# Log-sum-exp over rows: fewer GpSimd additions in the last rows, an early part of the range check, and other load sizes

## The chip, the cores and the metric

The kernel runs on one core of one Trainium2 chip. The metric is the device time of one execution in microseconds, lower is better. The time before is the median of three runs.

## The reference

For each of 32 x 512 = 16384 rows of 1024 numbers (fp32) the kernel returns the logarithm of the sum of the exponentials:

```python
"x": np.random.randn(32, 512, 1024).astype(np.float32)

def reference(x):
    max_x = np.max(x, axis=-1, keepdims=True)
    return (max_x.squeeze(-1) + np.log(np.sum(np.exp(x - max_x), axis=-1))).astype(np.float32)
```

## The kernel before

Each of the 128 partitions holds NC = 128 rows of 1024 elements. "Row 112" below means row 112 of every partition. The kernel takes the exponentials without the maximum, sums each row into one column of `sumexp`, and takes the logarithm. At the end it checks that all sums lie in a range in which that is exact enough; if they don't, a second path (not taken with these data) does everything again with the maximum.

The work is one long pipeline, written out by hand, with no scheduler: the order of the code is the order of each engine.

- SP issues 18 loads of x into a ring of 48 rows (`load`). A load waits until the sums that still read its place in the ring are done. The sizes and what is done with each load stand in the table `LOADS`: a size in rows, and then a list of parts.
- ScalarE waits for a load (`act.wait(landed[i], 16)`) and takes one exponential, in place, for each part of it.
- The sums of a part are made in one of these ways. **R**: VectorE reduces s whole rows with one `reduce_sum`. **G**: GpSimd adds the second half of each row onto its first half (`tensor_tensor`), and VectorE later reduces the halves (`sum_folded`), half the elements. **T**: VectorE adds both halves of one row and accumulates, one instruction a row (`add_halves`, two inputs). **a** is the first piece of the last row, summed by `add_halves`; **b** is the rest of the last row, which ScalarE itself accumulates while it takes the exponential.
- **H** in the list of parts calls `sum_folded` at once; without it this is done at the end of the load. **L** is the logarithm of the first 112 columns, which SP then stores. So in "G6 R10" VectorE reduces the ten whole rows and then the six half ones.

```python
    (16, "R16"), (16, "R16"), (16, "R16"), (16, "G6 R10"), (15.59375, "R9 G6"),
    ...
    (1.46875, "T1"), (1.0625, "T1"), (0.78125, "T1"), (0.59375, "T1+a"), (0.65625, "b"),
```

Behind the last load two things follow the last sum. On one side ScalarE takes the logarithms of columns 112 to 126 and of the last one, and SP stores these 16 columns. On the other side stands the range check: VectorE compares all 128 columns with the lower bound (`clamped`, `bad`) and sums them (`total`), TensorE adds these up over the partitions into one number (`count`, three products), and VectorE compares this with the upper bound (`fine`). ScalarE and VectorE load that truth value and branch; SP waits for both and for the store.

Of the kernel before, what the change touches and what calls it, by code (L numbers as in the profile page):

```python
# [9 lines left out]
LOW, HIGH = 1e-15, 1e15  # L10
# [4 lines left out]

LOADS = [
# [4 lines left out]
]  # L23


# [23 lines left out]
def kernel(  # L49
# [5 lines left out]
    nc = tc.nc  # L55
# [8 lines left out]
    AX = mybir.AxisListType  # L64
    ALU = mybir.AluOpType
# [4 lines left out]
    NC = n // P  # L70
    H = d // 2
# [8 lines left out]
    def source(e0, size):  # L80
        assert e0 >= W * d or e0 + size <= W * d
        return x_rest[:, e0 - W * d : e0 - W * d + size] if e0 >= W * d else x_rows[:, e0 : e0 + size]
# [4 lines left out]
        ])  # L87
        for size, parts in LOADS
    ]
    assert sum(size for size, _ in loads) == NC * d  # L90

    def sbuf(name, cols, dtype=fp32, rows=P):
        return nc.alloc_sbuf_tensor(name, [rows, cols], dtype).ap()

    ring = sbuf("ring", RING * d)
    sumexp = sbuf("sumexp", NC + 1)
    res = sbuf("res", NC)
    clamped = sbuf("clamped", NC)
    bad = sbuf("bad", 1)
    total = sbuf("total", 1)  # L100
    far = sbuf("far", 1)
    ones = sbuf("ones", 1)
    fine = sbuf("fine", 1, i32, 1)
    count = nc.alloc_psum_tensor("count", [1, 1], fp32).ap()
# [3 lines left out]
    dve = Counted(nc, nc.vector, "dve")  # L108
    pe = Counted(nc, nc.tensor, "pe")
    pool = Counted(nc, nc.gpsimd, "pool")  # L110
# [8 lines left out]
    constants = pool.did(nc.gpsimd.memset(far, 100 * HIGH))  # L119
# [4 lines left out]
    def load(i, here, done_before, size):  # L124
        for a, b, who, at in users:
            if a < here + size and b > here:
                sp.wait(who, at)
        users[:] = [u for u in users if not (u[0] < here + size and u[1] > here)]
        return nc.sync.dma_start(
            out=ring[:, here : here + size], in_=source(done_before, size)  # L130
        ).then_inc(landed[i], 16)

    c = 0
# [7 lines left out]
    def sum_folded():  # L141
        for c0, p0, s, at in folded:
            dve.wait(pool, at)
            half = ring[:, p0 : p0 + s * d].rearrange("p (c d) -> p c d", d=d)[:, :, 0:H]
            at = dve.did(nc.vector.reduce_sum(out=sumexp[:, c0 : c0 + s], in_=half, axis=AX.X))  # L145
            users.append((p0, p0 + s * d, dve, at))
            summed.append((c0, c0 + s, at))
        folded.clear()

    def add_halves(v, col):  # L150
        h = v.shape[-1] // 2
        lo = v[:, 0:h]
        return dve.did(nc.vector.scalar_tensor_tensor(  # L153
            out=lo, in0=lo, scalar=1.0, in1=v[:, h : 2 * h],
            op0=ALU.mult, op1=ALU.add, accum_out=sumexp[:, col : col + 1],
        ))

    for i, (size, parts) in enumerate(loads):
        if here + size > RING * d:
            assert here == p  # L160
            p = here = 0
        dma = load(i, here, done_before, size)
        first_load = first_load or dma.ins
        end = here + size
        done_before += size
        act.wait(landed[i], 16)
        for k, part in enumerate(parts):
            if part[0][0] == "H":
                sum_folded()
                continue  # L170
            if part[0][0] == "L":
                assert c >= W
                act.wait(dve, max(at for c0, _, at in summed if c0 < W))
                ln_early = act.did(nc.scalar.activation(  # L174
                    out=res[:, 0:W], in_=sumexp[:, 0:W], func=AF.Ln
                ))
                continue
            rows = sum(s for how, s in part if how in "RTG")
            more = any(q[0][0] not in "HL" for q in parts[k + 1 :])
            upto = p + rows * d if more else end  # L180
            v = ring[:, here:upto]
            if part[-1][0] == "b":
                last = act.did(nc.scalar.activation(  # L183
                    out=v, in_=v, func=AF.Exp, accum_out=sumexp[:, NC : NC + 1]
                ))
                here = upto
                continue
            at = act.did(nc.scalar.activation(out=v, in_=v, func=AF.Exp))  # L188
            here = upto
            for how, s in part:  # L190
                rows = ring[:, p : p + s * d].rearrange("p (c d) -> p c d", d=d)
                if how == "G":
                    pool.wait(act, at)
                    folded.append((c, p, s, pool.did(nc.gpsimd.tensor_tensor(  # L194
                        out=rows[:, :, 0:H], in0=rows[:, :, 0:H], in1=rows[:, :, H:d], op=ALU.add,
                    ))))
                elif how == "R":
                    dve.wait(act, at)
                    users.append((p, p + s * d, dve, dve.did(nc.vector.reduce_sum(  # L199
                        out=sumexp[:, c : c + s], in_=rows, axis=AX.X  # L200
                    ))))
                    summed.append((c, c + s, dve.n))
                elif how == "T":
                    dve.wait(act, at)
                    for r in range(s):
                        n_sums = add_halves(rows[:, r, :], c + r)
                        users.append((p + r * d, p + (r + 1) * d, dve, n_sums))
                        summed.append((c + r, c + r + 1, n_sums))
                elif how == "a":
                    dve.wait(act, at)  # L210
                    summed.append((LAST, NC, add_halves(ring[:, p:upto], LAST)))
                    s = 0
                c += s
                p += s * d
        sum_folded()
        assert here == end
# [5 lines left out]
    sums = dve.n  # L222
# [4 lines left out]
        out=res[:, LAST:NC], in_=sumexp[:, NC : NC + 1], func=AF.Ln, bias=sumexp[:, LAST:NC]  # L227
# [1 line left out]
    sp.wait(act, ln_last)  # L229
    nc.sync.dma_start(out=out_rest, in_=res[:, W:NC]).then_inc(stored, 16)  # L230

    dve.wait(dve, sums)
    dve.did(nc.vector.scalar_tensor_tensor(  # L233
        out=clamped, in0=sumexp[:, 0:NC], scalar=LOW, in1=sumexp[:, 0:NC],
        op0=ALU.max, op1=ALU.not_equal, accum_out=bad,
    ))
    at = dve.did(nc.vector.reduce_sum(out=total, in_=sumexp[:, 0:NC], axis=AX.X))  # L237
    pe.wait(pool, constants)
    pe.wait(dve, at)
    pe.did(nc.tensor.matmul(count, lhsT=bad, rhs=far, start=True, stop=False))  # L240
    pe.did(nc.tensor.matmul(count, lhsT=ones, rhs=total, start=False, stop=False))  # L241
    pe.wait(act, last)
    at = pe.did(nc.tensor.matmul(  # L243
        count, lhsT=ones, rhs=sumexp[:, NC : NC + 1], start=False, stop=True
    ))
    dve.wait(pe, at)
    at = dve.did(nc.vector.tensor_scalar(out=fine, in0=count, scalar1=HIGH, scalar2=None, op0=ALU.is_lt))  # L247
# [6 lines left out]
    with nc.If(all_fine < 1):  # L254
# [5 lines left out]
        for c0 in range(0, NC, RING):  # L260
# [6 lines left out]
            for c1, c2 in ((c0, edge), (edge, c0 + s)):  # L267
                if c1 == c2:
                    continue
                nc.scalar.dma_start(  # L270
                    out=ring[:, (c1 - c0) * d : (c2 - c0) * d],
                    in_=source(c1 * d, (c2 - c1) * d),
# [4 lines left out]
                out=neg, in_=v, op=ALU.max, axis=AX.X, negate=True  # L277
# [3 lines left out]
                out=v, in0=v, in1=neg[:, :, None].to_broadcast([P, s, d])  # L281
# [5 lines left out]
                out=sumexp[:, c0 : c0 + s], in_=v, axis=AX.X  # L287
# [71 lines left out]
```

## Time and profile before

| | us |
|---|---|
| median of 3 runs | 162.95 (162.81 to 163.07) |
| profiled execution | 163.12 |
| its span in the trace | 161.8 |
| VectorE busy | 116.0 (72%) |
| ScalarE busy | 115.0 (71%) |
| GpSimd busy | 42.3 (26%) |
| load queue's share of the 16 DMA engines' time | 97.0% |

The page shows one profiled execution. In its rows, L188 is ScalarE's exponential, L199 the reduction of whole rows (R), L145 the reduction of halves (after G), L153 the T sum, L194 GpSimd's addition, L233 and L237 the range check on VectorE, L129 the loads. Behind the arrow `<-` in brackets stands what the engine had waited for. A row "x16 | 90.0, 9001 | 42.3" gives the number of instructions, their busy time in us and mean ns, and the engine's idle time before them.

### The profile page before, as it was taken

Reading aid. Unit: us, or ns where it says so; the run is one execution under the profiler, and the core shown is the slowest. Engines: PE = TensorE matmul, PEld = TensorE weight load, DVE = VectorE, ACT = ScalarE, POOL = GpSimd, SP = SyncE. Lnnn points to the kernel's source line nnn. Section 1 sums busy time; section 2 is a strip of 40 time slices with the busy share of each in tenths; the row PEclk is TensorE's granted clock in tenths of the full one; section 3 lists DMA queues with packets and bytes.
Section 4 is the critical chain, followed back from the end, with each engine's and each line's share of the span. In section 5 each row is a group of like instructions: output and inputs, shape, how many; then the busy total and the mean of one; then the engine's idle time right before and its main releaser. Section 6 shows DMA issues by size and latency. Waiting matters only on the chain.

```text
span 161.8 us, 168 instructions
## 1 busy us (share of the span) xinstructions
PE 0.3 (0%) x6; PEld 0.2 (0%) x6; DVE 116.0 (72%) x40; ACT 115.0 (71%) x32; POOL 42.3 (26%) x16
## 2 busy tenths in 40 slices
PE   0000000000000000000000000000000000000000
PEld 0000000000000000000000000000000000000000
DVE  0000000019999499986999679999969999999996
ACT  3000069980899609993299915999998989899994
POOL 0000000000000000000009700002998299299830
DMA  8997997997998999799799598989998999999990
GB/s 292 486 518 308 470 519 324 454 518 340 437 518 356 421 519 437 340 518 454 317 505 505 253 505 370 543 381 424 434 434 356 440 448 412 420 414 427 417 368 3
DMA packets 2880, 67.18 MB, mean 415 GB/s; under 512 B 576, under 2 KB 576, under 8 KB 1344
## 3 DMA queue, kind: packets, MB, share of 16 engines
q1 hardware_dynamic: 2880, 67.18, 97.0%
HBM read 67.11 MB, written 0.07 MB: 415 GB/s over the span
## 4 chain that ended last, share of the span: by engine, by line
DMA 43%; DVE 30%; ACT 24%; POOL 1%; issue 0%; PE 0%
DMA ring<-in_x_dram 43%; ACT ring L188 24%; DVE sumexp L199 23%; DVE sumexp L145 4%; DVE ring L153 3%; POOL ring L194 1%; DVE clamped L233 0%; DVE total L237 0%; PE count L240 0%; DVE fine L247 0%; PE count L243 0%; PE count L241 0%
## 5 line engine op out<-in xcount | busy, mean ns | idle before, releaser
L188 ACT ACTIVATE ring<-ring 128x16384 f32<-128x16384 f32 (+21 forms) x26 | 112.3, 4373 | 42.9 <-DMA ring<-in_x_dram 42.9
L199 DVE TENSOR_REDUCE sumexp<-ring 128x16 f32<-128x16384 f32 (+6 forms) x10 | 90.0, 9001 | 42.3 <-ACT ring L188 42.2
L194 POOL TENSOR_TENSOR ring<-ring 128x3072 f32<-128x3072 f32 (+5 forms) x10 | 41.9, 4211 | 112.2 <-ACT ring L188 112.2
L145 DVE TENSOR_REDUCE sumexp<-ring 128x6 f32<-128x3072 f32 (+5 forms) x10 | 21.2, 2119 | 1.9 <-POOL ring L194 1.9
L153 DVE SCALAR_TENSOR_TENSOR ring<-ring 128x512 f32<-128x512 f32 (+1 forms) x8 | 5.4, 718 | 0.0
L117 ACT ACT_TABLE_LOAD x1 | 1.3, 1283 | 1.4 <-PEq L58 1.4
L183 ACT ACTIVATE ring<-ring 128x672 f32<-128x672 f32 x1 | 0.8, 764 | 0.1
L224 ACT ACTIVATE res<-sumexp 128x15 f32<-128x15 f32 x1 | 0.2, 214 | 0.6 <-DVE ring L153 0.6
L153 DVE DVE_READ_ACCUMULATOR ring<-ring 128x1 f32 x8 | 0.6, 78 | 0.0
L247 DVE TENSOR_SCALAR fine<-count 1x1 int32<-1x1 f32 x1 | 0.1, 147 | 0.5 <-PE count L243 0.5
L240 PE MATMUL count<-far,bad 128*1 128x1 f32 x2 | 0.2, 164 | 160.3 <-DVE total L237 160.3
L118 POOL MEMSET ones<- 128x1 f32 x1 | 0.1, 98 | 1.0 <-POOLq L58 1.0
L240 PEld LDWEIGHTS count<-far,bad 128*1 128x1 f32 x2 | 0.1, 79 | 160.3 <-issue 160.3
L233 DVE SCALAR_TENSOR_TENSOR clamped<-sumexp 128x128 f32<-128x128 f32 x1 | 0.3, 291 | 0.0
L237 DVE TENSOR_REDUCE total<-sumexp 128x1 f32<-128x128 f32 x1 | 0.3, 280 | 0.0
L174 ACT ACTIVATE res<-sumexp 128x112 f32<-128x112 f32 x1 | 0.3, 279 | 0.0
L226 ACT ACTIVATE res<-sumexp 128x1 f32<-128x1 f32 x1 | 0.3, 279 | 0.0
L241 PE MATMUL count<-total,ones 128*1 128x1 f32 x2 | 0.2, 164 | 0.0
L243 PE MATMUL count<-sumexp,ones 128*1 128x1 f32 x2 | 0.2, 162 | 0.0
L183 ACT ACTIVATION_READ_ACCUMULATOR ring<-ring 128x1 f32 x1 | 0.2, 186 | 0.0
L343 POOL MEMSET const-float32-0.0<- 128x1 f32 x1 | 0.1, 99 | 0.2 <-issue 0.2
L241 PEld LDWEIGHTS count<-total,ones 128*1 128x1 f32 x2 | 0.1, 82 | 0.0
(6 smaller groups left out, 0.6 us busy)
## 6 DMA issues: line engine op xcount, KB each, us to landing
ring<-in_x_dram SPq DMA_DIRECT2D x1, 7984.0 KB, 26.4
ring<-in_x_dram SPq DMA_DIRECT2D x1, 5840.0 KB, 20.8
ring<-in_x_dram SPq DMA_DIRECT2D x1, 4480.0 KB, 15.2
ring<-in_x_dram SPq DMA_DIRECT2D x1, 3472.0 KB, 23.3
ring<-in_x_dram SPq DMA_DIRECT2D x1, 2800.0 KB, 20.7
ring<-in_x_dram SPq DMA_DIRECT2D x1, 2080.0 KB, 20.8
ring<-in_x_dram SPq DMA_DIRECT2D x1, 1456.0 KB, 24.0
ring<-in_x_dram SPq DMA_DIRECT2D x1, 1328.0 KB, 26.7
```

The lines of the kernel that those rows point to most:

```text
L117: nc.scalar.preload_act_table_set("natural_log_exp_and_others")
L145: at = dve.did(nc.vector.reduce_sum(out=sumexp[:, c0 : c0 + s], in_=half, axis=AX.X))
L153: return dve.did(nc.vector.scalar_tensor_tensor(out=lo, in0=lo, scalar=1.0, in1=v[:, h : 2 * h], op0=ALU.mult, op1=ALU.add, accum_out=sume ...
L174: ln_early = act.did(nc.scalar.activation(out=res[:, 0:W], in_=sumexp[:, 0:W], func=AF.Ln))
L183: last = act.did(nc.scalar.activation(out=v, in_=v, func=AF.Exp, accum_out=sumexp[:, NC : NC + 1]))
L188: at = act.did(nc.scalar.activation(out=v, in_=v, func=AF.Exp))
L194: folded.append((c, p, s, pool.did(nc.gpsimd.tensor_tensor(out=rows[:, :, 0:H], in0=rows[:, :, 0:H], in1=rows[:, :, H:d], op=ALU.add,))))
L199: users.append((p, p + s * d, dve, dve.did(nc.vector.reduce_sum(out=sumexp[:, c : c + s], in_=rows, axis=AX.X))))
L226: ln_last = act.did(nc.scalar.activation(out=res[:, LAST:NC], in_=sumexp[:, NC : NC + 1], func=AF.Ln, bias=sumexp[:, LAST:NC]))
L233: dve.did(nc.vector.scalar_tensor_tensor(out=clamped, in0=sumexp[:, 0:NC], scalar=LOW, in1=sumexp[:, 0:NC], op0=ALU.max, op1=ALU.not_equal ...
L240: pe.did(nc.tensor.matmul(count, lhsT=bad, rhs=far, start=True, stop=False))
L241: pe.did(nc.tensor.matmul(count, lhsT=ones, rhs=total, start=False, stop=False))
```

## The change

- `LOADS` has other sizes behind row 64, and other parts behind row 48. Loads stay 18, and the ninth still ends at row 112.
- GpSimd's last addition is row 118's. Before, it also added row 122; rows 115 to 117, too, are split differently: before, 115 was an R and 116 and 117 were Gs; after, 114 and 115 are Gs, 116 and 117 Ts. There are ten T sums instead of seven. An H stands in four places, so that sums of halves come ahead of the following R or T.
- A new part **C** sums the folded halves and then checks the columns so far (0 to 113) with `check(0, 0, 114)`: the same two VectorE instructions and two of the three matmuls, now in the tenth load. At the end `check(1, 114, 128)` does the other 14 columns. VectorE comes to it behind the sum of rows 112 and 113 and ahead of that of rows 114 and 115. In its first instruction both inputs are `sumexp`.
- The logarithm L moves from the end of the eleventh load to the end of the twelfth.

```diff
-    (16, "R16"), (16, "R16"), (16, "R16"), (16, "G6 R10"), (15.59375, "R9 G6"),
-    (11.40625, "G5 R7"), (8.75, "G6 R2"), (6.78125, "G3 R4"), (5.46875, "G4 R2"),
-    (4.0625, "G3 R1"), (2.84375, "G2 L"), (2.59375, "G1 T2"), (1.9375, "T1 G1"),
-    (1.46875, "T1"), (1.0625, "T1"), (0.78125, "T1"), (0.59375, "T1+a"), (0.65625, "b"),
+    (16, "R16"), (16, "R16"), (16, "R16"), (16, "G6 H R10"), (14.40625, "R9 G5"),
+    (11.59375, "G3 R5 R4"), (9.3125, "G3 H R6"), (6.875, "G4 R3"), (5.8125, "G2 H R4"),
+    (2.96875, "G2 C"), (3.5, "G2 H T2"), (2.65625, "G1 T2 L"), (1.46875, "T1"),
+    (1.6875, "T2"), (1.28125, "T1"), (0.9375, "T1"), (0.75, "T1+a"), (0.75, "b"),
...
+    def check(k, c0, c1):
+        dve.wait(dve, dve.n)
+        dve.did(nc.vector.scalar_tensor_tensor(
+            out=clamped[:, c0:c1], in0=sumexp[:, c0:c1], scalar=LOW, in1=sumexp[:, c0:c1],
+            op0=ALU.max, op1=ALU.not_equal, accum_out=bad[:, k : k + 1],
+        ))
+        at = dve.did(nc.vector.reduce_sum(
+            out=total[:, k : k + 1], in_=sumexp[:, c0:c1], axis=AX.X
+        ))
+        if k == 0:
+            pe.wait(pool, constants)
+        pe.wait(dve, at)
+        pe.did(nc.tensor.matmul(count, lhsT=bad[:, k : k + 1], rhs=far, start=k == 0, stop=False))
+        pe.did(nc.tensor.matmul(count, lhsT=ones, rhs=total[:, k : k + 1], start=False, stop=False))
...
+            if part[0][0] == "C":
+                sum_folded()
+                checked = c
+                check(0, 0, c)
+                continue
...
-    dve.wait(dve, sums)
-    dve.did(nc.vector.scalar_tensor_tensor(
-        out=clamped, in0=sumexp[:, 0:NC], scalar=LOW, in1=sumexp[:, 0:NC],
-        op0=ALU.max, op1=ALU.not_equal, accum_out=bad,
-    ))
-    at = dve.did(nc.vector.reduce_sum(out=total, in_=sumexp[:, 0:NC], axis=AX.X))
-    pe.wait(pool, constants)
-    pe.wait(dve, at)
-    pe.did(nc.tensor.matmul(count, lhsT=bad, rhs=far, start=True, stop=False))
-    pe.did(nc.tensor.matmul(count, lhsT=ones, rhs=total, start=False, stop=False))
+    check(1, checked, NC)
```

More of the change, by code (lines that the diff above doesn't have):

```diff
@@ L98 @@
     clamped = sbuf("clamped", NC)
-    bad = sbuf("bad", 1)
-    total = sbuf("total", 1)
+    bad = sbuf("bad", 2)
+    total = sbuf("total", 2)
     far = sbuf("far", 1)
@@ L178 @@
             rows = sum(s for how, s in part if how in "RTG")
-            more = any(q[0][0] not in "HL" for q in parts[k + 1 :])
+            more = any(q[0][0] not in "HLC" for q in parts[k + 1 :])
             upto = p + rows * d if more else end
```

## The prediction

> **What bounds the kernel now.** I read the page first, then the chain of waits in order of time, then groups by form for durations, and the timeline behind 138 us.
>
> ```profile
> PE 0.3 (0%) x6; PEld 0.2 (0%) x6; DVE 116.0 (72%) x40; ACT 115.0 (71%) x32; POOL 42.3 (26%) x16
> ...
> DMA 43%; DVE 30%; ACT 24%; POOL 1%; issue 0%; PE 0%
> ```
>
> No engine is full over the span, and the chain has a stretch of each. So what counts is who ends last in which stretch. Stretches by the windows view (columns: PE, PEld, DVE, ACT, POOL busy, clock, DMA share, GB/s), then the chain (start, length, what):
>
> ```profile
> 79.80:138.30 58.50, 0.00 (x0) 0.00 (x0) 54.42 (x9) 51.43 (x10) 28.69 (x5) 1.00 0.98 421
> 138.30:158.20 19.90, 0.00 (x0) 0.00 (x0) 19.73 (x21) 19.47 (x15) 13.26 (x6) 1.00 0.96 400
> ```
>
> ```profile
> 117.62 20.70 DMA ring<-in_x_dram
> ...
> 138.35 11.22 ACT ring L188 x5
> 149.57 0.07 issue
> 149.64 2.37 POOL ring L194
> ...
> 152.03 1.22 DVE sumexp L145
> ```
>
> The loads stream without a pause (share 0.98, then 0.96), so row 112 is in at 138.32 (117.62 + 20.70) and nothing before that can pull the end. From there five exponentials, one GpSimd addition and then VectorE without a gap set the end. In the last 19.9 us VectorE is busy 19.73 and ScalarE 19.47: the tail is balanced and VectorE ends last. Where exactly it ends (timeline; start, length):
>
> ```profile
> 153.16 0.68 DVE L153 SCALAR_TENSOR_TENSOR ring<-ring 128x512 f32<-128x512 f32 x1
> 154.38 0.68 DVE L145 TENSOR_REDUCE sumexp<-ring 128x1 f32<-128x512 f32 x1
> 154.50 1.27 POOL L194 TENSOR_TENSOR ring<-ring 128x512 f32<-128x512 f32 x1 [1.27 <-ACT ring L188]
> 154.98 1.33 DVE L153 SCALAR_TENSOR_TENSOR ring<-ring 128x512 f32<-128x512 f32 x1
> 157.45 0.68 DVE L153 SCALAR_TENSOR_TENSOR ring<-ring 128x512 f32<-128x512 f32 x1
> 158.06 0.68 DVE L153 SCALAR_TENSOR_TENSOR ring<-ring 128x512 f32<-128x512 f32 x1
> 158.19 0.76 ACT L183 ACTIVATE ring<-ring 128x672 f32<-128x672 f32 x1
> 158.86 0.19 ACT L183 ACTIVATION_READ_ACCUMULATOR ring<-ring 128x1 f32 x1
> 159.29 0.33 DVE L153 SCALAR_TENSOR_TENSOR ring<-ring 128x176 f32<-128x176 f32 x1
> 159.66 0.29 DVE L233 SCALAR_TENSOR_TENSOR clamped<-sumexp 128x128 f32<-128x128 f32 x1
> 159.88 0.28 DVE L237 TENSOR_REDUCE total<-sumexp 128x1 f32<-128x128 f32 x1
> 160.08 0.34 SPq L230 DMA_DIRECT2D out_dram<-res  x1
> ```
>
> Three things are to be seen. VectorE ends its last sum at 159.62 (159.29 + 0.33); call this X. ScalarE's last accumulator is out at 159.05, 0.57 earlier. And the T sum at 154.98 took 1.33 instead of 0.68: it ran beside a GpSimd addition (154.50 to 155.77) and ended 0.54 behind that one's end, so it had stood until 156.31 - 0.68 = 155.63. A T sum (two inputs in the ring) waits for a GpSimd addition in flight; the reduction at 154.38, one input, overlaps the same addition and keeps its 0.68.
>
> That is the place for a rule. The Trainium skill (SBUF — State Buffer, Who interferes with whom) says that VectorE instructions with two SBUF inputs share a port pair with GpSimd instructions that read SBUF, that the one that starts first holds it for its whole length and the other fully blocks, and that reductions never contend. These rows agree, with 0.65 us lost once.
>
> **What follows X.** The range check (0.29 and 0.28) and the last store run side by side.
>
> ```profile
> SPq L303 <- DVEq L300: 1.2, 1, 1.2
> ```
>
> ```profile
> out_dram<-res SPq DMA_DIRECT2D x1, 8.0 KB, 1.4
> ```
>
> The store, issued at 160.08, lands 1.4 later, at about 161.5. SP has issued it by 160.42 and then waits 1.2 for VectorE's branch behind the check (first row), until about 161.65; the span ends at 161.8. So the check is last, by 0.1 to 0.2.
>
> **The change, part by part.** Durations (groups by form; the number before the last bar's end is the mean ns):
>
> ```profile
> L199 DVE TENSOR_REDUCE sumexp<-ring 128x10 f32<-128x10240 f32 x1 | 10.8, 10819 | 2.2 <-ACT ring L188 2.2
> L145 DVE TENSOR_REDUCE sumexp<-ring 128x6 f32<-128x3072 f32 x3 | 10.1, 3350 | 1.8 <-POOL ring L194 1.8
> L199 DVE TENSOR_REDUCE sumexp<-ring 128x4 f32<-128x4096 f32 x1 | 4.4, 4409 | 0.0
> L145 DVE TENSOR_REDUCE sumexp<-ring 128x3 f32<-128x1536 f32 x2 | 3.5, 1741 | 0.0
> L145 DVE TENSOR_REDUCE sumexp<-ring 128x2 f32<-128x1024 f32 x1 | 1.2, 1221 | 0.2 <-POOL ring L194 0.2
> L188 ACT ACTIVATE ring<-ring 128x1504 f32<-128x1504 f32 x1 | 1.4, 1441 | 0.0
> L188 ACT ACTIVATE ring<-ring 128x2048 f32<-128x2048 f32 x1 | 1.9, 1893 | 0.0
> L188 ACT ACTIVATE ring<-ring 128x3072 f32<-128x3072 f32 x1 | 2.8, 2763 | 0.0
> L194 POOL TENSOR_TENSOR ring<-ring 128x1024 f32<-128x1024 f32 x1 | 2.4, 2356 | 0.1
> ```
>
> *Load sizes.* Rows 64 to 112 come in five loads before and after, and row 112 ends the ninth load in both; sixteen later rows come in nine loads in both. So I keep 138.32 and a last landing just before 158.19. Loads of other sizes at the same count and bytes could shift either by some tenths, in either direction; 0.2 of that goes into the range.
>
> *VectorE up to row 112.* The H behind the first G6 puts its sum ahead of R10. What stood there before:
>
> ```profile
> 74.41 17.22 DVE L199 TENSOR_REDUCE sumexp<-ring 128x16 f32<-128x16384 f32 x1 [2.14 <-ACT ring L188]
> 85.27 6.72 POOL L194 TENSOR_TENSOR ring<-ring 128x3072 f32<-128x3072 f32 x1 [83.69 <-ACT ring L188]
> ```
>
> VectorE was free at 91.63 and then idle for 2.2 (last column of the R10 row); the GpSimd addition was ready at 91.99. After, it starts at 92.02. Then come, by element count, 3072, 10240, 9216, 2560, 5120, 4096, 1536, 1536, 6144, 3072, 2048, 1024, 4096: 3.35 + 10.82 + 9.75 + 2.81 + 5.48 + 4.41 + 1.74 + 1.74 + 6.55 + 3.35 + 2.28 + 1.22 + 4.41 = 57.91 (sizes without a row lie on the line between their neighbours). Successive ones overlap by 0.08 (the reduction at 154.38 takes 0.68, the next instruction starts at 154.98), so 13 times 0.08 off: the sum of rows 112 and 113 can start at 148.89. No idle time in between: at each step the producer is ahead, nearest for the G5 addition behind R9, by about 0.1. This stretch also frees the ring: the loads that wait for these sums are issued by about 118.5 and 130, over 15 us before the stream reaches them. The store of the first 112 rows goes behind ScalarE's later logarithm, some 2.5 us later; it queues behind loads already issued, and nobody waits for it before the end.
>
> *ScalarE and GpSimd behind row 112.* After the landing at 138.32 come exponentials of 1856, 4096 and 3040 elements: on the line through the three rows 1.73 + 3.63 + 2.74, less two overlaps of 0.08: 138.35 + 7.94 = 146.29. GpSimd adds rows 112 and 113 from 146.36 (0.07 of issue in the chain) to 148.72, and rows 114 and 115 at once behind it, to about 151.05 (joined additions overlap by some 0.03). VectorE sums 112 and 113 at 148.9 and is done by 150.1.
>
> *The early check.* Its first instruction reads `sumexp` twice: the two-input kind. VectorE reaches it at 150.15, in the middle of the second addition. No row shows this instruction beside a GpSimd addition. Bounds: nothing, as it then hides in the wait for that addition, which the next sum (114, 115) has anyway; or it stands until 150.91 (0.14 before the addition's end, as the T sum did). I take the second, by the row at 154.98. Then 0.22 to the reduction (159.66 to 159.88) and 0.20 to the next: the sum of 114 and 115 starts at 151.33 instead of 151.08, a cost of 0.25. The early matmuls lie beside this, on an idle engine. By the rule of the Trainium skill named above (SBUF — State Buffer, Who interferes with whom) the check is held like the T sum, and the sum comes to 162.5; without the rule it would be 162.3.
>
> *T instead of G.* A T sum costs 0.61 a row, and the half sum of a single row behind a G costs 0.60 (154.38 to 154.98). So row 122 moves off GpSimd for 0.01, and the 0.65 stall at 154.98 goes. From 151.33: 1.13 for the sum (152.03 to 153.16), ten T sums of 0.61 (158.06 less 157.45) and the sum of row 118 (0.60): 7.83, so part a starts at 159.16. It has 128 elements: 0.33 less 48 times (0.68 - 0.33)/336, 0.28. X is 159.44, against 159.62: **-0.18**. GpSimd's last addition, row 118, ends near 152.3, just before the first T sum at 152.46. Next late is ScalarE's last accumulator, with 96 more elements at about 159.13 (159.05 + 0.08); it has 0.31 to spare.
>
> *The late check.* 14 columns instead of 128: 114 elements at the same slope are 0.12 less, twice: 0.24 off the check's path. The store's path keeps its length and then ends with it, so the gain is **-0.23**, give or take 0.1.
>
> Sum: -0.41 against the profiled execution. That took 163.12 with its span of 161.8, 0.17 above the median of the runs, 162.95; I take the difference over: 162.95 - 0.41 = 162.54, in round numbers **162.5**.
>
> **Rivals.** *The check is not held.* If the two-input read of 114 short elements doesn't meet GpSimd, the 0.25 goes: 162.3. For it: nothing but the different operand. Against: the row at 154.98.
>
> *The check is held through two additions.* At 151.05 GpSimd has row 118 ready (its exponential is done by about 150.2), and its additions follow each other without a gap: four took 11.64 in one piece.
>
> ```profile
> 141.59 11.64 POOL L194 TENSOR_TENSOR ring<-ring 128x2048 f32<-128x2048 f32 x4 [2.86 <-ACT ring L188]
> ```
>
> If GpSimd takes the ports again before VectorE, the check stands for that addition's 1.27 (the row at 154.50) as well, and everything behind it moves by as much: -0.41 + 1.27 = +0.86, **163.8**. It decides wherever the second addition is queued when the first ends. The page says who waits but not who is next; VectorE had asked first, and so I hold it the less likely.
>
> *The stream sets the end.* If a landing of the new ladder is 0.3 late, at row 112 or at the last load, the 0.18 is lost and only part of the late check's gain remains: 162.8. For it: ScalarE's margin of only 0.31, and GpSimd's chain, which starts at row 112's landing and has none. Against: equal numbers of loads.
>
> **Chances.** Held once, 0.57 (its own range 162.3 to 162.8); not held, 0.10; held twice, 0.17; stream, 0.13; anything else, 0.03. The range from 162.1 to 163.2 leaves out the check held twice, 0.17, and little more. About what a measurement can tell from no change is 0.2%, 0.33 us: the first two cases less a small part of the first give faster 0.62; the stream's case and that part 0.17; slower 0.21.
>
> **What would show it.** The early check's first instruction lasting about 0.9 to 1.0 us and ending near a GpSimd addition's end; no T sum over 0.7; VectorE's last sum at 159.4; the late check about 0.24 shorter; the last store landing level with the check. It would be wrong if the early check ended behind row 118's addition (near 152.3), if VectorE idled between 92 and 148, or if ScalarE's last exponential started behind 158.4.

## The result, and the profile after

| | us |
|---|---|
| before, median of 13 runs | 163.00 (162.67 to 163.22) |
| changed, median of 13 runs | 162.59 (162.44 to 162.77) |
| ratio to before | 0.9977, 95% interval 0.9969 to 0.9986 |
| forecast | 162.5, range 162.1 to 163.2 |
| span of the profiled execution, before and after | 161.8 and 161.2 |

The change makes the kernel faster by 0.23%, 0.41 us. The spans of the two profiled executions lie further apart, by 0.6: in the first one the load that ends at row 112 came late (see "The kernel before, profiled again"). The page of the changed kernel, engines and chain by engine:

```profile
span 161.2 us, 183 instructions
...
PE 0.5 (0%) x10; PEld 0.3 (0%) x10; DVE 119.1 (74%) x48; ACT 115.1 (71%) x32; POOL 32.4 (20%) x15
...
DVE 53%; DMA 30%; ACT 12%; POOL 4%; PE 0%; issue 0%
```

GpSimd gave up 9.9 us of busy time and VectorE took 3.1. The chain in order of time:

```profile
85.25 6.72 POOL ring L215
91.97 0.02 issue
92.00 3.35 DVE sumexp L146
95.35 20.39 DVE sumexp L220 x2
...
148.87 1.14 DVE sumexp L146
150.00 0.02 issue
150.03 0.78 DVE clamped L161 x2
150.80 0.18 DVE total L165
150.99 1.13 DVE sumexp L146
...
155.16 3.89 DVE ring L154 x14
```

From 92.00 to the last check's second instruction the chain stays on VectorE: the sum that the first H moved starts at 92.00, and rows 112 and 113 are summed from 148.78. The timeline around the early check and at the end:

```profile
145.98 5.95 POOL L215 TENSOR_TENSOR ring<-ring 128x1024 f32<-128x1024 f32 x3 [3.77 <-ACT ring L209]
...
150.03 0.77 DVE L161 SCALAR_TENSOR_TENSOR clamped<-sumexp 128x114 f32<-128x114 f32 x1
150.73 0.08 DVE L161 DVE_READ_ACCUMULATOR clamped<-sumexp 128x1 f32 x1
150.73 0.26 DVE L165 TENSOR_REDUCE total<-sumexp 128x1 f32<-128x114 f32 x1
150.91 1.20 DVE L146 TENSOR_REDUCE sumexp<-ring 128x2 f32<-128x1024 f32 x1
...
152.04 0.67 DVE L154 SCALAR_TENSOR_TENSOR ring<-ring 128x512 f32<-128x512 f32 x1
...
158.01 0.84 ACT L204 ACTIVATE ring<-ring 128x768 f32<-128x768 f32 x1
...
158.75 0.28 DVE L154 SCALAR_TENSOR_TENSOR ring<-ring 128x128 f32<-128x128 f32 x1
158.76 0.19 ACT L204 ACTIVATION_READ_ACCUMULATOR ring<-ring 128x1 f32 x1
...
159.07 0.17 DVE L161 SCALAR_TENSOR_TENSOR clamped<-sumexp 128x14 f32<-128x14 f32 x1
...
159.17 0.16 DVE L165 TENSOR_REDUCE total<-sumexp 128x1 f32<-128x14 f32 x1
...
159.50 0.34 SPq L251 DMA_DIRECT2D out_dram<-res  x1
...
159.71 0.15 DVE L259 TENSOR_SCALAR fine<-count 1x1 int32<-1x1 f32 x1 [0.38 <-PE count L255]
```

The early check's first instruction took 0.77 for 114 columns; the same one over 14 columns takes 0.17 and over 128 took 0.29. It stood, and it stands in the row as a long instruction, not as idle time. The chain of waits doesn't show it either: it names VectorE and not GpSimd, whose second addition ends at 150.66. No T sum is longer than 0.68. VectorE's last sum ends at 159.03 (158.75 + 0.28), and ScalarE's last accumulator is out at 158.95 (158.76 + 0.19), 0.08 earlier.

### The profile page after: what moved, and what is told of

Read it like the earlier page. It is cut to its first block, busy times and chain, and to the rows that moved or that the text cites. A ratio compares the mean times of both kernels' runs of the same rounds, so it can differ in the third digit from the quotient of the medians.

```text
span 161.2 us, 183 instructions
## 1 busy us (share of the span) xinstructions
PE 0.5 (0%) x10; PEld 0.3 (0%) x10; DVE 119.1 (74%) x48; ACT 115.1 (71%) x32; POOL 32.4 (20%) x15
## 4 chain that ended last, share of the span: by engine, by line
DVE 53%; DMA 30%; ACT 12%; POOL 4%; PE 0%; issue 0%
DVE sumexp L220 38%; DMA ring<-in_x_dram 30%; ACT ring L209 12%; DVE sumexp L146 10%; POOL ring L215 4%; DVE ring L154 4%; DVE clamped L161 1%; DVE total L165 0%; PE count L171 0%; DVE fine L259 0%; PE count L255 0%; PE count L172 0%
## 5 line engine op out<-in xcount | busy, mean ns | idle before, releaser
L209 ACT ACTIVATE ring<-ring 128x16384 f32<-128x16384 f32 (+22 forms) x26 | 112.4, 4371 | 42.7 <-DMA ring<-in_x_dram 42.6
L220 DVE TENSOR_REDUCE sumexp<-ring 128x16 f32<-128x16384 f32 (+6 forms) x10 | 96.1, 9639 | 40.0 <-ACT ring L209 40.0
L215 POOL TENSOR_TENSOR ring<-ring 128x1024 f32<-128x1024 f32 (+5 forms) x9 | 32.1, 3573 | 118.3 <-ACT ring L209 118.3
L146 DVE TENSOR_REDUCE sumexp<-ring 128x2 f32<-128x1024 f32 (+5 forms) x9 | 16.1, 1802 | 0.4 <-POOL ring L215 0.4
L154 DVE SCALAR_TENSOR_TENSOR ring<-ring 128x512 f32<-128x512 f32 (+1 forms) x11 | 6.5, 642 | 0.0
L161 DVE SCALAR_TENSOR_TENSOR clamped<-sumexp 128x114 f32<-128x114 f32 (+1 forms) x2 | 0.9, 472 | 0.1
L204 ACT ACTIVATE ring<-ring 128x768 f32<-128x768 f32 x1 | 0.8, 843 | 0.1
```

The source lines that it names most:

```text
L154: return dve.did(nc.vector.scalar_tensor_tensor(out=lo, in0=lo, scalar=1.0, in1=v[:, h : 2 * h], op0=ALU.mult, op1=ALU.add, accum_out=sume ...
L161: dve.did(nc.vector.scalar_tensor_tensor(out=clamped[:, c0:c1], in0=sumexp[:, c0:c1], scalar=LOW, in1=sumexp[:, c0:c1], op0=ALU.max, op1=A ...
L204: last = act.did(nc.scalar.activation(out=v, in_=v, func=AF.Exp, accum_out=sumexp[:, NC : NC + 1]))
L215: folded.append((c, p, s, pool.did(nc.gpsimd.tensor_tensor(out=rows[:, :, 0:H], in0=rows[:, :, 0:H], in1=rows[:, :, H:d], op=ALU.add,))))
```

## The experiments

Eleven runs. Each ratio is to the kernel before, timed on the same chip in the same session. "The changed kernel" is the one of the prediction.

**The changed kernel again.**

> The changed kernel unaltered, in one more execution with a profile. Two readings of its trace are at stake. Row 112 landed at 138.00 instead of 138.32: if the load sizes do that, it lands at 138.0 again, within 0.1; if it is chance of one execution, it may land anywhere from 137.9 to 138.4. VectorE's branch at the end took 0.49 us from its comparison's end to its next semaphore, 0.15 before the change: if that is the program's (where its code lies), it is 0.49 again and the span stays at 161.2; if it is chance, it is near 0.15 and the span about 160.9, with the store then last.

0.9977 (0.9967 to 0.9987), median 162.59. Row 112 landed (its load had arrived) at 138.05, and VectorE's branch again took 0.49. The early landing looked like an effect of the load sizes, until the kernel before was profiled again (below).

**The early check one load earlier.**

```diff
-(6.875, "G4 R3"), (5.8125, "G2 H R4"), (2.96875, "G2 C"),
+(6.875, "G4 R3"), (5.8125, "G2 C R4"), (2.96875, "G2"),
```

> The early check stands one load earlier, ahead of R4 of rows 108 to 111, over 108 columns instead of 114; there no GpSimd addition runs (142.21 to 145.98 it is idle). Theory (the check's cost is the hold by the addition of rows 114 and 115): its first instruction takes 0.27 instead of 0.77, its 0.45 disappears in the 0.68 that VectorE waits for that addition anyway, the sum of rows 114 and 115 starts at 150.69 instead of 150.91, VectorE ends 0.22 earlier, at about 158.8, and the time is 0.2 less than the changed kernel's, ScalarE's last accumulator at 158.95 being next. Rival (the check costs VectorE its own 0.45 wherever it stands): no change against the changed kernel, VectorE's last sum at 159.03.

0.9969 (0.9958 to 0.9980), median 162.40 (runs from 162.26 to 162.56), against 162.59 for the changed kernel beside it (162.52 to 162.80). VectorE's timeline in this kernel:

```profile
144.51 0.27 DVE L161 SCALAR_TENSOR_TENSOR clamped<-sumexp 128x108 f32<-128x108 f32 x1
...
149.22 1.21 DVE L146 TENSOR_REDUCE sumexp<-ring 128x2 f32<-128x1024 f32 x1
150.60 1.22 DVE L146 TENSOR_REDUCE sumexp<-ring 128x2 f32<-128x1024 f32 x1 [0.18 <-POOL ring L215]
```

0.27 instead of 0.77, and the sum of rows 114 and 115 now waits for GpSimd itself. VectorE's last sum ends 20.84 behind the landing of row 112 (158.74 less 137.90), against 21.03 in the changed kernel: 0.19 for 0.22 expected. The theory holds: beside an addition the early check costs VectorE 0.19, as most of its hold falls into a wait for GpSimd that comes anyway. One load earlier it costs nothing: without any early check (next experiment) the last sum ends 20.84 behind the landing, too.

**One check at the end.**

```diff
-(2.96875, "G2 C"),
+(2.96875, "G2"),
...
-    check(1, checked, NC)
+    check(0, 0, NC)
```

> The check is one again, over all 128 columns at the end; everything else is as in the changed kernel. Theory (the early part costs 0.22 on the path and saves 0.24 behind the last sum): VectorE's last sum is 0.22 earlier, at about 158.8, the late check is 0.24 longer, and the time is that of the changed kernel within 0.1. Rival 1 (the early part is hidden, the split is worth all of 0.24): VectorE's last sum stays at 159.0 and the time is 0.24 more. Rival 2 (the split is worth nothing because the store is last anyway): the time is 0.2 less.

0.9990 (0.9979 to 1.0000), median 162.75: 0.16 more than the changed kernel, between the theory and the first rival. The runs of the two overlap (162.63 to 162.96 here, 162.52 to 162.80 there), so the 0.16 is known only to about 0.1, an estimate from these spreads. VectorE's timeline:

```profile
148.83 1.21 DVE L146 TENSOR_REDUCE sumexp<-ring 128x2 f32<-128x1024 f32 x1
150.73 1.22 DVE L146 TENSOR_REDUCE sumexp<-ring 128x2 f32<-128x1024 f32 x1 [0.69 <-POOL ring L215]
...
158.91 0.29 DVE L161 SCALAR_TENSOR_TENSOR clamped<-sumexp 128x128 f32<-128x128 f32 x1
...
159.12 0.28 DVE L165 TENSOR_REDUCE total<-sumexp 128x1 f32<-128x128 f32 x1
159.88 0.15 DVE L259 TENSOR_SCALAR fine<-count 1x1 int32<-1x1 f32 x1 [0.47 <-PE count L255]
```

Without the early check the sum of rows 114 and 115 waits 0.69 for GpSimd, so VectorE had that much to spare. The last sum ends 0.19 earlier behind the landing, as expected. But from the late check's start to the truth value's start there are now 0.97 us (158.91 to 159.88) and in the changed kernel 0.64 (159.07 to 159.71). So the split saves 0.33 and not 0.24. The missing 0.09 lies ahead of TensorE's first product. In the chains, first here and then in the changed kernel, this stands between the sum of `total` and that product:

```profile
159.41 0.14 issue
```

```profile
159.34 0.04 issue
```

The changed kernel's first products have run by then (at 151.13). A cost of 0.19 and a worth of 0.33 leave 0.14, against 0.16 in the times.

**GpSimd adds row 122 again.**

```diff
-    (1.6875, "T2"), (1.28125, "T1"),
+    (1.6875, "G1 T1"), (1.28125, "T1"),
```

> Row 122's halves are added on GpSimd again (its load is G1 T1 instead of T2), the rest as in the changed kernel. Theory (a T sum meets GpSimd's addition and one of them stands): the addition becomes ready at about 154.1, waits for the T sum then running until about 154.5, and holds the next T sum until about 155.6; that T sum takes 1.2 instead of 0.68, VectorE ends 0.5 later and the time is 0.4 to 0.5 more than the changed kernel's. If the addition starts at once, beside the T sum, the hold is only 0.1. Rival (the hold seen before the change was chance, and only the count of VectorE's instructions matters): the time is that of the changed kernel within 0.05, as the half sum of one row costs 0.60 and its T sum 0.61.

1.0053 (1.0036 to 1.0070), median 163.82: 1.23 more than the changed kernel, over twice what the theory said. The timeline:

```profile
153.38 0.68 DVE L154 SCALAR_TENSOR_TENSOR ring<-ring 128x512 f32<-128x512 f32 x1
153.88 1.30 POOL L215 TENSOR_TENSOR ring<-ring 128x512 f32<-128x512 f32 x1 [1.83 <-ACT ring L209]
153.99 0.08 DVE L154 DVE_READ_ACCUMULATOR ring<-ring 128x1 f32 x1
153.99 1.75 DVE L154 SCALAR_TENSOR_TENSOR ring<-ring 128x512 f32<-128x512 f32 x1
```

The addition became ready at 153.88, before the T sum of 153.99. It did not wait for the T sums in a row to end: it took its turn when the one of 153.38 ended, and the next stood 1.07 longer than its 0.68. I had the addition ready only at 154.1, in the middle of that next T sum. VectorE's last sum ends 22.08 behind the landing instead of 21.03, 1.05 later; the other 0.2 of the times is not explained. The rival falls: the same count of sums costs over 1 us more when one addition comes among them. How long a T sum is held depends on when the addition starts. Here that is 0.11 ahead of the T sum, and the hold is 1.07. In the kernel before it was 0.48 ahead (154.50 and 154.98), and the hold 0.65.

**The kernel before, profiled again.**

> The kernel before, unaltered, profiled once more. Row 112 landed at 138.32 in its first profile and at 137.90 to 138.12 in five profiles of kernels with the new load sizes. If the sizes do that, it lands at 138.3 again, within 0.1. If that one execution was late by chance, at 138.0 or so, and then the sum over VectorE ends some 0.3 earlier than 159.62. VectorE's branch again takes 0.15 to its next semaphore.

ScalarE starts on the load that ends at row 112 at 138.13 (landing 138.11), 0.2 earlier than in the first profile, and VectorE's last sum ends at 159.32, 0.30 earlier.

```profile
154.20 1.27 POOL L194 TENSOR_TENSOR ring<-ring 128x512 f32<-128x512 f32 x1 [1.15 <-ACT ring L188]
...
154.81 1.21 DVE L153 SCALAR_TENSOR_TENSOR ring<-ring 128x512 f32<-128x512 f32 x1
```

So 138.32 was the chance of one execution, and 0.2 of the difference between the first two profiles is not the change's. The three other profiles with the old loads up to row 112 (below) have 138.07 to 138.11, the seven with the new ones 137.90 to 138.16. The stalled T sum is there again (1.21).

**The loads up to row 112 alone.** Everything behind row 112 as before the change, with one check at the end.

```diff
-    (2.96875, "G2 C"), (3.5, "G2 H T2"), (2.65625, "G1 T2 L"), (1.46875, "T1"),
-    (1.6875, "T2"), (1.28125, "T1"), (0.9375, "T1"), (0.75, "T1+a"), (0.75, "b"),
+    (4.0625, "G3 R1"), (2.84375, "G2 L"), (2.59375, "G1 T2"), (1.9375, "T1 G1"),
+    (1.46875, "T1"), (1.0625, "T1"), (0.78125, "T1"), (0.59375, "T1+a"), (0.65625, "b"),
```

> The new loads and parts of rows 48 to 112 alone; from row 112 on the loads and parts of the kernel before, and one check over 128 columns at the end. Theory (the head brings row 112 in 0.3 earlier and no more; the tail brings the rest): the T sum of row 121 stands beside GpSimd's addition of row 122 as before (1.3), VectorE's last sum ends near 159.3, 0.3 before that of the kernel before and 0.2 to 0.3 behind that of the changed kernel. Its time lies 0.1 to 0.3 under the kernel before. Rival (the head does nothing, 138.32 was chance): the time of the kernel before, within 0.1.

1.0016 (1.0007 to 1.0025), median 163.26. Neither: this part of the change makes the kernel slower, by 0.2 us. Row 112 landed at 138.16, so it brought nothing in earlier, and VectorE's last sum ended at 159.49, 21.33 behind the landing. VectorE waits for GpSimd here, in front of the sum of rows 116 and 117:

```profile
152.08 1.22 DVE L146 TENSOR_REDUCE sumexp<-ring 128x2 f32<-128x1024 f32 x1 [0.24 <-POOL ring L215]
```

In the second profile of the kernel before it did not wait there.

**The loads behind row 112 alone, twice.**

```diff
-    (16, "R16"), (16, "R16"), (16, "R16"), (16, "G6 H R10"), (14.40625, "R9 G5"),
-    (11.59375, "G3 R5 R4"), (9.3125, "G3 H R6"), (6.875, "G4 R3"), (5.8125, "G2 H R4"),
+    (16, "R16"), (16, "R16"), (16, "R16"), (16, "G6 R10"), (15.59375, "R9 G6"),
+    (11.40625, "G5 R7"), (8.75, "G6 R2"), (6.78125, "G3 R4"), (5.46875, "G4 R2"),
```

> Loads and parts of the kernel before up to row 112, and those of the changed kernel behind it, with its split check. Theory (the head's part of the gain is the 0.3 at row 112's landing): row 112 lands at 138.3, VectorE's last sum ends near 159.2 to 159.35, with ScalarE's last accumulator close, and the time is 0.2 to 0.3 more than the changed kernel's. Rival (the whole gain is in the tail): the time of the changed kernel within 0.1.

0.9954 (0.9940 to 0.9967), median 162.30: faster than the changed kernel, which neither reading had said.

> The kernel with the old loads up to row 112 and the new ones behind it, once more, beside the changed kernel on the same chip: the first time had 5 undisturbed runs. If its lead over the changed kernel (0.9954 against 0.9977 of the kernel before) is real, it is 0.2 to 0.4 faster than the changed kernel again; if not, the two lie within 0.1.

0.9957 (0.9944 to 0.9970), median 162.35; the changed kernel beside it 162.62. These five runs (162.26 to 162.45) and the eight beside them (162.55 to 162.74) don't overlap: the lead is real, 0.27 us. No kernel that ran has a lower ratio to the kernel before; the interval of the one with the early check one load earlier (0.9958 to 0.9980) overlaps with it, and the two were not combined.

> The changed kernel, to stand beside the other two on the same chip: 162.6, or 0.9977 of the kernel before. Row 112 at 138.0 to 138.1 and VectorE's last sum 21.0 behind it.

0.9974 (0.9964 to 0.9984); landing 138.06, last sum 21.03 behind it.

**Why the loads up to row 112 cost something.** The kernel above with one boundary moved:

```diff
-(6.78125, "G3 R4"), (5.46875, "G4 R2"),
+(6.4375, "G3 R4"), (5.8125, "G4 R2"),
```

> As the kernel with the old loads up to row 112, but the boundary between its last two loads there lies 0.34 rows earlier (6.4375 and 5.8125 rows instead of 6.78125 and 5.46875), so that the load that ends at row 112 is as long as in the changed kernel; the parts stay. Theory (what the new loads up to row 112 cost is the 352 elements more that ScalarE has left when row 112 lands: 0.29 on the chain to GpSimd's second addition): that addition ends 0.29 later, the early check is held 0.29 longer (0.7 instead of 0.4), VectorE ends near 159.2 instead of 158.9, and the time is 0.2 to 0.3 more, that of the changed kernel. Rival (the order of the sums ahead of row 112 costs it): the time with the old boundary, within 0.1.

0.9979 (0.9971 to 0.9988), median 162.75: 0.40 more than with the old boundary, and level with the changed kernel (162.62) within the intervals. The early check's first instruction with the old boundary, and then with the moved one:

```profile
150.33 0.37 DVE L161 SCALAR_TENSOR_TENSOR clamped<-sumexp 128x114 f32<-128x114 f32 x1
```

```profile
150.17 0.72 DVE L161 SCALAR_TENSOR_TENSOR clamped<-sumexp 128x114 f32<-128x114 f32 x1
```

0.72 instead of 0.37, and VectorE ends 21.11 instead of 20.82 behind the landing, 0.29 as the theory has it. The rest of the 0.40 isn't in the spans (161.3 and 161.1) and stays open. So the load that ends at row 112 is what matters there, and the rival falls. What ScalarE has left to do when that row lands goes, through GpSimd's two additions, straight to VectorE. The changed kernel makes that load 5.81 rows instead of 5.47.

**Eight more instructions on VectorE.**

```diff
+    for k in range(8):
+        dve.did(nc.vector.memset(clamped[:, k : k + 1], 0.0))
```

> The kernel before with eight VectorE memsets of one column each at its start, while VectorE waits for the first load anyway (35.7 us idle): the changed kernel's VectorE has eight instructions more ahead of its branch, too. If VectorE's branch is slow because of where its code lies, it takes 0.49 to the next semaphore here as well, the check ends 0.34 later and the time is 0.3 more than the kernel before's. If it is slow for another reason (the values, the wait), it takes 0.15 and the time is that of the kernel before.

1.0004 (0.9995 to 1.0013): no measurable difference in time. But the branch took 0.50, and SP's wait for it grew from 1.2 to 1.6:

```profile
SPq L306 <- DVEq L303: 1.6, 1, 1.6
```

The branch and the semaphore behind it, first in the second profile of the kernel before and then with the memsets (the times at the end are where it starts):

```profile
L299 DVEq COMPARE_BRANCH  x1: 67/67/67, 161.1 to 161.1; - x1
L300 DVEq EVENT_SEMAPHORE  x1: 21/21/21, 161.3 to 161.3; - x1
```

```profile
L302 DVEq COMPARE_BRANCH  x1: 67/67/67, 161.1 to 161.1; - x1
L303 DVEq EVENT_SEMAPHORE  x1: 21/21/21, 161.7 to 161.7; - x1
```

So the slower branch follows the number of instructions ahead of it. The eleven runs have spans from 161.7 to 161.9, those of the kernel before beside them 161.3 to 161.7; the medians of the times are 163.13 and 163.05. The span grew by about 0.3 and the time, by its interval, by at most 0.2. Why the two differ, the runs don't show.

## Why the prediction was right

*The bound and the places.* VectorE ended last, at 159.03 for 159.44 forecast. Counted from the landing of row 112, it is 21.03 for 21.12. The sum of rows 112 and 113 was to start at 148.89 and started at 148.78. ScalarE's last accumulator had 0.08 to spare in this profile and 0.30 in the two others of the changed kernel, for 0.31 forecast.

*The likeliest case.* The check was held once. GpSimd had row 118's addition ready and started it in the row of three from 145.98, but VectorE had its turn between the two additions; the check's first instruction ended at 150.80. So the rival of two additions didn't occur. The instruction lasted 0.77 and not the 0.9 to 1.0 forecast: row 112, and with it the addition's end, came 0.3 to 0.4 earlier than forecast, VectorE only 0.1. The price in VectorE's last sum was 0.19 for 0.25. "Not held" is refuted by the row, and by the experiment that moved the check to a place without an addition, which won the 0.19. The Trainium skill's rule (SBUF — State Buffer, Who interferes with whom) holds here for 114 elements as for 512.

*The T sums.* The stall of 0.65 (0.53 in the second profile) is gone and no T sum is held. Putting the one addition back costs 1.2.

*X.* The forecast was -0.18 at an equal landing. From the landings, the kernel before ends its last sum 21.29 and 21.21 behind, the changed one 21.03 in all three profiles: -0.18 to -0.26.

*The late check* is the term that was mis-sized, twice, with opposite signs. The path from the late check's start to the truth value's got 0.33 shorter (0.97 to 0.64 us) and not 0.24. VectorE's branch then took 0.34 longer, which the prediction did not have. In the span the stretch behind X is therefore as long as before (2.2 us to its end). The store lands 1.9 behind X in both kernels.

*The total.* Of the measured 0.41, X explains about 0.2. The rest matches the -0.23 of the prediction in size, but no trace shows it in the place where the prediction put it. Two runs bear on it. With one check at the end the time is 0.16 more, so between kernels that both have the slow branch the shorter check counts. With the memsets the slow branch alone costs no measurable time. Together they would let the late check have the remaining 0.2, but that is an argument: no kernel with the split check and the fast branch ran. That the total agrees to a hundredth is luck, as the terms behind X do not agree that well.

*The load sizes.* "I keep 138.32" was off by 0.3, mostly from an accident of one profile: the sizes don't move the landing by more than the spread between executions. What was wrong in the step was to look only at when row 112 lands. The 352 elements more in its load were in my sum as an exponential of 4096 elements behind one of 1856, but I never asked what the old boundary would have given. It would have been 0.27 us faster.

## What to carry to other kernels

In these profiles an instruction that is held by another engine appears as a long one, not as a wait: compare it with its own kind at the same size, and look at what the other engine was doing at that moment. Here a single addition of 1.30 among a row of two-input sums cost over 1 us, so the price of moving one is read from when it becomes ready and not from busy time. And a change with several parts deserves a run of each half: here one half was worth 0.75 us and the other took about 0.3 of it back.

## What the runs showed that I had not expected

VectorE's branch at the end took 0.15 from the comparison's end to the next semaphore in three profiles (the kernel before, twice, and the one with the new loads up to row 112 alone). It took 0.49 to 0.50 in all others, in which VectorE has more instructions ahead of it (45 to 48 on the page instead of 40 or 41), and eight memsets in an idle stretch are enough. The Trainium skill (Runtime: NRT & Kernel Launch, Instruction fetch mechanics) says that a taken branch whose target lies outside the current window of fetched instructions must wait until the target has been fetched; the dependence on the count agrees with that, but no run here shows the fetch itself. The time of the runs did not follow it (1.0004), so a third of a microsecond in a span of this kernel need not be one of the measured time.

When GpSimd and VectorE both had work queued, the turn went from one to the other, in both directions: VectorE's check went between two additions, and the addition of row 122 between two T sums. Taking turns is one reading of this. The other is that whoever asked first goes first: the check stood from 150.03, ahead of the addition of row 118, and row 122's addition was ready at 153.88, ahead of the T sum of 153.99. The runs don't part the two.
